# Gate and up weights of two column tiles summed and split during the out-projection, stored split in DRAM and loaded by their visits

## The chip, the cores and the metric

The kernel runs on one core of one Trainium2 chip. The metric is device microseconds of one execution; the time of a kernel is the median of several runs. A separate execution is taken with the hardware profiler, and all rows below come from that one.

## What is computed

One layer of a hybrid backbone on 1024 latent and 128 context tokens of width 1024: a mixer (differential attention, a bidirectional recurrence, a Fourier mixing) with one output projection, and then a SwiGLU feed-forward network. The part around the change is:

```python
x = x + g1 * rmsnorm(mixer_parts @ w_out, g_post_mix)
h = rmsnorm(x, g_pre_ffn) * (1.0 + sc2) + sh2
gt, up = split(h @ w_gate_up)          # two halves of 2816 columns
f = (silu(gt) * up) @ w_down
x = x + g2 * rmsnorm(f, g_post_ffn)
```

## The kernel before, in words

Every fp32 product is made of three matmuls on split operands: a high part (`copy` on ACT, L169, rounds to fp32r) and a low part (`lo` on DVE, L175, subtracts the high part). `mm3` (L185 to L187) multiplies high by low, high by high and low by high.

**Out-projection.** Nine token tiles of 128 tokens, each 12.1 us of TensorE. The loop `for t, ki in opg` (L1438) gets a turn after every second contraction step, so ki runs from 0 to 7 in a tile. After tile t come, in program order: squares of its two halves on ACT (`oproj_sq`, L1092), a reciprocal root on POOL (`rstd2`, L1083 and L1084), scaling and the residual sum on DVE (`oproj_post1`, L1098 and L1100) with squares on ACT (L1101), a second `rstd2`, and a scaling on DVE (`oproj_post2`, L1111). At ki 7 of the next tile TensorE transposes the result (`h2_turn`, L1409, tile `ot`); it stands in TensorE's queue between two tiles, so the next tile's matmuls wait for it. DVE and ACT then modulate it (`h2_mod`, L1424 and L1421, tile `ou`), split it into the operand `av` (`token_operands1`, `token_operands2`) and POOL forms sums of its quarters (`token_sums`, L1393 to L1396).

**Gate and up.** The product uses seven block products in place of eight (a Strassen scheme). A visit v is a column tile g of 128 gate and 128 up columns times one or two chunks of tokens: chunk 0 has 320 columns per matmul, chunk 1 has 256. Visits 0, 1 and 2 take tiles 0, 1 and 2 with chunk 0 alone, since chunk 1 is not ready; their chunk 1 comes in visits 6, 9 and 12. All other visits take both chunks (`VIS`, L1332). A visit has seven products of 12 matmuls per chunk. Its weights are a raw tile of 1 MB (`raw`, two buffers, `load_gu`), three sums on POOL (`weight_sums`, L1356 to L1358, into `t3`, `t2` and the raw tile), a fourth on POOL (L1374) and seven splits, one per product, by `prep(q)`: q counts products, 7 to a visit. A split goes to one of seven slots (`slots`, tile name `gu`). `prep` runs four products ahead of the product that uses it, and products 0 to 3 are prepared in the last two tiles of the out-projection.

**The order.** The order of each engine is the order of the code; the framework adds the waits. All DMAs but one are issued from SP's queue, in program order, and a DMA that waits holds back those behind it. In the gate and up stage the same queue carries the stores of hidden tiles (`HB<-hf`, L1556) and, in full visits, loads and stores of summed weights for the later stage (`tw`, `WT<-tw`, L1586 and L1596; POOL's L1593 and L1594 come just ahead of the stores).

Of the kernel before, what the change touches and what calls it, by code (L numbers as in the profile page):

```python
# [9 lines left out]
F32 = mybir.dt.float32  # L10
# [6 lines left out]
P = 128  # L17
D = 1024
# [135 lines left out]
def _body(tc, nc, A):  # L154
# [7 lines left out]
    def rdma(eng, out, in_):  # L162

        f = lambda v: v.bitcast(F32) if v.dtype == F32R else v
        eng.dma_start(f(out), f(in_))
# [28 lines left out]
    ML = tc.dram_tile([D, T], F32, name="ML")  # L194
    X1 = tc.dram_tile([T, D], F32, name="X1")
    HB = tc.dram_tile([NT, P, NJ, P], F32, name="HB")
    HS = [tc.dram_tile([8, P, NK, P], F32, name=f"HS{i}") for i in range(2)]
    WT = tc.dram_tile([NK, P, 4 * 512], F32, name="WT")
    H2B = tc.dram_tile([2, P, D], F32, name="H2B")
# [607 lines left out]
    for i in range(2, NU):  # L807
        ps = mm.tile([P, 3, 512], F32, name=f"pu{i}", tag="mm")
        w = wsl.pop(i)
# [533 lines left out]
    avp = pool("av", side="right", reuse_waits="tile")  # L1343
    AV = [[avp.tile([P, 7, 4, CN[0]], F32R, name=f"av0{h}") for h in range(2)]]

    def load_gu(v):
        SP.dma_start(raw[v % 2].rearrange("p a c -> p (a c)"), A["w_gu"][VIS[v][0]])

    PRODS = (0, 3, 1, 4, 6, 2, 5)

    def weight_sums(v):

        r = raw[v % 2]
        POOL.tensor_tensor(t3, r[:, 1, 512:], r[:, 1, :512], op=OP.subtract)  # L1356
        POOL.tensor_tensor(t2, t3, r[:, 0, :512], op=OP.add)
        POOL.tensor_tensor(r[:, 1, :512], r[:, 1, :512], r[:, 0, :512], op=OP.subtract)  # L1358

    def prep(q):  # L1360

        v, p = divmod(q, 7)
        if v >= NV_:
            return
        r = raw[v % 2]
        if q == 0:
            weight_sums(0)
        b11, b21, b12, b22 = r[:, 0, :512], r[:, 0, 512:], r[:, 1, :512], r[:, 1, 512:]
        src = (b11, t2, b21, t3, b12, b21, b22)[p]
        w = slots[q % NS]  # L1370
        copy(ACT, w[:, 0], src)
        lo(w[:, 1], src, w[:, 0])
        if p == 2:
            POOL.tensor_tensor(b21, b21, t2, op=OP.subtract)  # L1374
        elif p == 5 and v + 1 < NV_:
            weight_sums(v + 1)
        elif p == 6 and v + 2 < NV_:
            load_gu(v + 2)

    def token_split(dst, u, i, vs, src):  # L1380
        c = slice(64 * i, 64 * i + 64)
# [46 lines left out]
        SP.dma_start(H2B[t - PT[0]], hu[t].rearrange("p a k c -> p (a k c)"))  # L1428

    load_mix(2)  # L1430
    oproj_sq(0, 0)
    oproj_sq(0, 1)
    rstd2(ovec[:, 0])
# [4 lines left out]
    for t, ki in opg:  # L1438
        if ki == 6 and t + 2 < NT:
            load_mix(t + 2)  # L1440
        if t > 1 and ki == 3:
            oproj_sq(t, 0)
        if t == 2 and ki in HK0:
            h2_turn(0, HK0.index(ki))
            if ki == HK0[1]:
                h2_mod(0, 0)
                h2_mod(0, 1)
                token_operands1(AV[0], hu[0], 0)
                token_sums(hu[0])
        if (t, ki) == (2, KO2):  # L1450
            token_operands2(AV[0], hu[0], 0)
        for q in range(2):
            if t > 1 and ki == HK[q]:
                h2_turn(t - 1, q)
        if ki == 7:
            oproj_sq(t, 1)
            rstd2(ovec[:, t])
            if t > 1:
                h2_mod(t - 1, 0)
                h2_mod(t - 1, 1)  # L1460
                if PT[0] <= t - 1 < 7:
                    h2_store(t - 1)
            oproj_post1(t)
            if 2 < t < PT[0] + 2:
                token_operands2(AV[0], hu[t - 2], t - 2)
            if 1 < t <= PT[0]:
                token_operands1(AV[0], hu[t - 1], t - 1)
            oproj_post2(t)
            if 1 < t <= PT[0]:
                token_sums(hu[t - 1])  # L1470
            if t + 2 < NT:
                load_x1in(t + 2)
        if t == 6 and ki == 0:
            load_gu(0)
        if t >= 7 and ki in (2, 4) and 2 * (t - 7) + (ki == 4) < NS0:
            prep(2 * (t - 7) + (ki == 4))

# [410 lines left out]
```

## Time and profile before

| what | value |
|---|---|
| median of 3 runs (lowest to highest) | 1401.82 us (1400.85 to 1402.37) |
| the profiled execution's own time | 1395.38 us |
| its span in the profile | 1393.6 us |
| TensorE, VectorE, ScalarE, GpSimd busy share | 96%, 63%, 43%, 42% |
| mean share of the 16 DMA engines, SP's queue | 53.6% |
| transposes behind the out-projection's last tile | 638.3 us |
| visits 0, 1 and 2 | 639.1 to 689.3 us |

Starts in the trace are microseconds from the span's start. A row of the timeline gives start, duration, engine, line, operation, output and inputs, and in brackets the idle time before it with what ended it. Matmuls overlap, so their durations are longer than the distance between their starts; the distance is what counts.

### The profile page before, as it was taken

How to read it: one execution, taken by the hardware profiler on the slowest of the kernel's cores; microseconds unless marked ns; L12 is line 12 of the kernel's file. 1: busy time of each engine (PE TensorE's matmuls, PEld its weight loads, DVE VectorE, ACT ScalarE, POOL GpSimd, SP SyncE). 2: the span in 40 equal slices, each digit the busy share in tenths (PEclk: the TensorE clock that was granted, in tenths of full speed). 3: DMA queues.
4: the chain of work that ended last, by engine and by line, in shares of the span. 5: the costliest groups of instructions: out<-in, count | busy, mean ns of one | idle time of the engine just before them, and what ended most of it. 6: DMA issues, size and time to landing. Idle time of an engine off the chain costs nothing.

```text
span 1393.6 us, 22864 instructions
## 1 busy us (share of the span) xinstructions
PE 1343.8 (96%) x8786; PEld 1225.4 (88%) x8786; DVE 877.1 (63%) x1302; ACT 593.2 (43%) x1176; POOL 582.1 (42%) x523
## 2 busy tenths in 40 slices
PE   7999999998999999999899999999999999999997
PEld 6887789798898888888799999999999998888886
DVE  5824444672788872666887777767666666555564
ACT  7511226643788883546423332322222245343431
POOL 2301111230576672444766666668665532010111
PEclk9999999999999999999999999999999999999999
DMA  8567751148654525563254544557454479546564
GB/s 323 193 210 268 243 192 46 38 144 198 170 145 111 143 61 170 172 220 139 95 178 171 186 150 142 168 205 232 153 165 128 144 233 316 182 171 200 172 236 143
DMA packets 156342, 242.41 MB, mean 174 GB/s; under 512 B 9253, under 2 KB 113098, under 8 KB 152778
## 3 DMA queue, kind: packets, MB, share of 16 engines
q1 hardware_dynamic: 156090, 240.44, 53.6%
q8 instruction: 69, 1.13, 0.3%
q10 hardware_dynamic: 144, 0.52, 0.1%
q14 instruction: 39, 0.32, 0.1%
HBM read 172.62 MB, written 68.31 MB: 173 GB/s over the span
## 4 chain that ended last, share of the span: by engine, by line
PE 49%; DVE 2%; issue 1%; ACT 1%; POOL 0%; DMA 0%; DVEq 0%; POOLq 0%; ACTq 0%
PE g L187 11%; PE g L185 11%; PE g L186 11%; PE d L185 6%; PE d L187 6%; PE d L186 6%; DVE gu L175 1%; DVE av L175 0%; DVE u L1533 0%; ACT gu L169 0%; DMA raw_gu<-in_w_down 0%; DVE hf L1533 0%; ACT av L169 0%; DVE hd L175 0%; ACT hd L169 0%
## 5 line engine op out<-in xcount | busy, mean ns | idle before, releaser
L187 PE MATMUL g<-av,gu 128*128 128x320 f32 (+1 forms) x1232 | 364.2, 296 | 7.7 <-DVE gu L175 7.4
L185 PE MATMUL g<-av,gu 128*128 128x320 f32 (+1 forms) x1232 | 364.3, 296 | 1.2 <-ACT av L169 0.8
L186 PE MATMUL g<-av,gu 128*128 128x320 f32 (+1 forms) x1232 | 363.1, 295 | 0.0
L187 PEld LDWEIGHTS g<-av,gu 128*128 128x128 f32 x1232 | 232.1, 188 | 10.3 <-DVE gu L175 10.2
L185 PEld LDWEIGHTS g<-av,gu 128*128 128x128 f32 x1232 | 231.9, 188 | 2.3 <-issue 1.4
L186 PEld LDWEIGHTS g<-av,gu 128*128 128x128 f32 x1232 | 232.2, 188 | 0.0
L175 DVE TENSOR_TENSOR gu<-raw_gu,gu 128x512 fp32r<-128x512 f32 x149 | 162.6, 1104 | 36.8 <-ACT gu L169 36.8
L185 PE MATMUL pu<-hl,w 128*128 128x384 f32 x336 | 123.0, 366 | 3.3 <-POOL hl L175 2.6
L187 PE MATMUL pu<-hh,w 128*128 128x384 f32 x336 | 113.3, 337 | 0.0
L186 PE MATMUL pu<-hh,w 128*128 128x384 f32 x336 | 113.1, 337 | 0.0
L185 PE MATMUL d<-dw,hd 128*128 128x512 f32 x244 | 95.7, 392 | 0.8 <-DVE dw L175 0.8
L943 PE MATMUL s<-ks,qs 128*128 128x384 f32 x384 | 91.6, 360 | 4.5 <-DMA ks<-KL 2.6
L187 PE MATMUL d<-dw,hd 128*128 128x512 f32 x244 | 95.6, 392 | 0.0
L186 PE MATMUL d<-dw,hd 128*128 128x512 f32 x244 | 95.3, 390 | 0.0
L1533 DVE TENSOR_TENSOR u<-g,u 128x320 f32<-128x320 f32 (+1 forms) x176 | 77.1, 448 | 26.8 <-PE g L187 26.7
L949 DVE TENSOR_REDUCE nm<-s 128x1 f32<-128x1152 f32 x64 | 86.6, 1353 | 9.8 <-PE s L943 9.6
L956 ACT ACTIVATE p<-s,nm 128x1152 f32<-128x1152 f32 x64 | 78.2, 1222 | 29.2 <-DVE nm L949 16.1
L169 ACT ACTIVATE gu<-raw_gu 128x512 fp32r<-128x512 f32 x149 | 88.7, 620 | 4.5 <-DMA raw_gu<-WT 2.9
L185 PEld LDWEIGHTS pu<-hl,w 128*128 128x128 f32 x336 | 63.5, 189 | 20.4 <-issue 13.7
L997 PE MATMUL o<-av,th 128*128 128x128 f32 x576 | 79.8, 275 | 0.0
L1552 ACT ACTIVATE u<-u 128x576 f32<-128x576 f32 (+2 forms) x26 | 15.9, 612 | 143.2 <-DVE u L1533 143.2
L997 PEld LDWEIGHTS o<-av,th 128*128 128x128 f32 x576 | 73.8, 191 | 0.2
(292 smaller groups left out, 2908.7 us busy)
## 6 DMA issues: line engine op xcount, KB each, us to landing
raw_gu<-in_w_gu SPq DMA_DIRECT2D x25, 1024.0 KB, 5.0
wmb<-in_w_mod SPq DMA_DIRECT2D x32, 512.0 KB, 5.2
tw<-in_w_down SPq DMA_DIRECT2D x22, 512.0 KB, 6.0
WT<-tw SPq DMA_DIRECT2D x22, 512.0 KB, 2.7
HS<-sa SPq DMA_DIRECT2D x22, 512.0 KB, 4.0
hr<-HS SPq DMA_DIRECT2D x16, 704.0 KB, 5.0
hr<-HB SPq DMA_DIRECT2D x15, 704.0 KB, 4.2
HB<-hf SPq DMA_DIRECT2D x18, 576.0 KB, 4.5
```

Of the source, the lines that this page charges most:

```text
L169: ACT.activation(out, in_, AF.Copy)
L175: eng.tensor_tensor(out, x, hi.bitcast(F32), op=OP.subtract)
L185: PE.matmul(out, wh, xl, start=first, stop=False)
L186: PE.matmul(out, wh, xh, start=False, stop=False)
L187: PE.matmul(out, wl, xh, start=False, stop=last)
L943: PE.matmul(b[:, j, :CW], q[:, st_, m, i * P:(i + 1) * P], ks[:, m, j * CW:(j + 1) * CW], start=(st_ == 0), stop=(st_ == 1))
L949: DVE.tensor_reduce(nm, s, axis=AX.XY, op=OP.max, negate=True)
L956: ACT.activation(p.rearrange("p (n c) -> p n c", c=CW), s, AF.Exp, bias=nm, accum_out=ss)
L997: PE.matmul(d["o"], d["t", g][:, i * P:(i + 1) * P], v[:, 3 * g + i], start=(g == 0 and i == 0), stop=(g == 2 and i == 2))
L1533: add = lambda out, x: DVE.tensor_tensor(out, b, x, op=OP.add)
L1552: ACT.activation(tmp("u3"), tmp("u3"), AF.Silu)
```

## The change

The sums and splits of column tiles 0 and 1 are made once, in the out-projection. A generator `early_gen` is advanced at ki 1, 3 and 5 of tiles 2 to 8: one step makes the three sums, each of the next seven makes one split into slot 2 or 3 by turns and stores it (512 KB) to a new DRAM tensor `WP`; with the seventh split of tile 0 the raw tile is loaded again, for column tile 1. The 17th step, in tile 7, loads the raw weights of the first visit that still splits. In visits 0, 1, 6 and 9 `prep` is a load of 512 KB from `WP` into the slot; the other visits are as before.

```diff
+    WP = tc.dram_tile([2, 7, P, D], F32, name="WP")
...
-    def load_gu(v):
-        SP.dma_start(raw[v % 2].rearrange("p a c -> p (a c)"), A["w_gu"][VIS[v][0]])
+    NPRE = 2
+    REAL = [v for v in range(NV_) if VIS[v][0] >= NPRE]
+
+    def load_raw_gu(r, g):
+        SP.dma_start(r.rearrange("p a c -> p (a c)"), A["w_gu"][g])
+
+    def load_gu(i):
+        if i < len(REAL):
+            load_raw_gu(raw[i % 2], VIS[REAL[i]][0])
...
+    def split_gu(r, p, w):
         b11, b21, b12, b22 = r[:, 0, :512], r[:, 0, 512:], r[:, 1, :512], r[:, 1, 512:]
         src = (b11, t2, b21, t3, b12, b21, b22)[p]
-        w = slots[q % NS]
         copy(ACT, w[:, 0], src)
         lo(w[:, 1], src, w[:, 0])
         if p == 2:
             POOL.tensor_tensor(b21, b21, t2, op=OP.subtract)
-        elif p == 5 and v + 1 < NV_:
-            weight_sums(v + 1)
-        elif p == 6 and v + 2 < NV_:
-            load_gu(v + 2)
+
+    def prep(q):
+        v, p = divmod(q, 7)
+        if v >= NV_:
+            return
+        w, g = slots[q % NS], VIS[v][0]
+        if g < NPRE:
+            rdma(SP, w, WP[g, p].rearrange("p (a c) -> p a c", a=2))
+        else:
+            i = REAL.index(v)
+            split_gu(raw[i % 2], p, w)
+            if p == 6:
+                load_gu(i + 2)
+        if p == 5 and v + 1 in REAL:
+            weight_sums(raw[REAL.index(v + 1) % 2])
+
+    def early_gen():
+        for g in range(NPRE):
+            weight_sums(raw[0])
+            yield
+            for p in range(7):
+                w = slots[2 + p % 2]
+                split_gu(raw[0], p, w)
+                rdma(SP, WP[g, p].rearrange("p (a c) -> p a c", a=2), w)
+                if p == 6 and g + 1 < NPRE:
+                    load_raw_gu(raw[0], g + 1)
+                yield
+        load_gu(0)
+        yield
...
     load_mix(2)
+    load_raw_gu(raw[0], 0)
+    early = early_gen()
...
-        if t == 6 and ki == 0:
-            load_gu(0)
+        if t > 1 and ki in (1, 3, 5):
+            next(early, None)
         if t >= 7 and ki in (2, 4) and 2 * (t - 7) + (ki == 4) < NS0:
             prep(2 * (t - 7) + (ki == 4))
```

What the diff does not show is where the new instructions fall among those of the out-projection. Three places matter. In the rows the lines are those of each kernel's own file (a line of the new kernel stands one to some thirty lines further down), and a name's first number is the token tile or the slot.

First ACT in tile 3, before, from the squares of tile 3's first half:

```order
L1092 ACTIVATE tm3_6072,ovec_3334<-op30_6046 128x512
L1092 ACTIVATE tm3_6072,ovec_3334<-op31_6047 128x512
L1421 ACTIVATE ou2_6115<-ot21_6107,M_83,S2_85 128x2x64
L1421 ACTIVATE ou2_6115<-ot21_6107,M_83,S2_85 128x2x64 x3
L1101 ACTIVATE tm3_6072,ovec_3334<-x13_5916 128x512
```

and now:

```order
L169 ACTIVATE gu2_5841<-raw_gu0_5836 128x512
L1093 ACTIVATE tm3_6087,ovec_3335<-op30_6057 128x512
L169 ACTIVATE gu3_5842<-t3_5838 128x512
L169 ACTIVATE gu2_5841<-raw_gu0_5836 128x512
L1093 ACTIVATE tm3_6087,ovec_3335<-op31_6058 128x512
L1448 ACTIVATE ou2_6136<-ot21_6128,M_84,S2_86 128x2x64
```

The second copy into slot `gu2` stands ahead of the squares of tile 3's second half (`op31`), and it may start only when the store of what the first copy and its DVE row left in `gu2` has landed. Tiles 5 and 6 have the same pattern.

Second POOL in tile 4, before:

```order
L1395 TENSOR_TENSOR ou2_6115<-ou2_6115 128x256
L1396 TENSOR_TENSOR ou2_6115<-ou2_6115 128x256
L1083 TENSOR_SCALAR ovec_3334<-ovec_3334 128x1
L1084 TENSOR_TENSOR ovec_3334<-ovec_3334,mhalf_82 128x1
L1083 TENSOR_SCALAR ovec_3334<-ovec_3334 128x1
```

and now:

```order
L1422 TENSOR_TENSOR ou2_6136<-ou2_6136 128x256
L1423 TENSOR_TENSOR ou2_6136<-ou2_6136 128x256
L1365 TENSOR_TENSOR t3_5838<-raw_gu0_5836 128x512
L1366 TENSOR_TENSOR t2_5837<-t3_5838,raw_gu0_5836 128x512
L1367 TENSOR_TENSOR raw_gu0_5836<-raw_gu0_5836 128x512
L1084 TENSOR_SCALAR ovec_3335<-ovec_3335 128x1
L1085 TENSOR_TENSOR ovec_3335<-ovec_3335,mhalf_83 128x1
```

The three sums of column tile 1 have come between the sums of token tile 2 and the first `rstd2` of tile 4 (`ovec`); they wait for the raw tile, whose load SP issues behind the stores of the sixth and seventh split.

Third SP around the end of visit 5, before:

```order
L1347 DMA raw_gu1_6640<-in_w_gu 128x2048
L1596 DMA WT_74<-tw20_7598 128x1024
L1596 DMA WT_74<-tw21_7599 128x1024
L1556 DMA HB_71<-hf5_7665 128x9x128
```

and now:

```order
L165 DMA gu2_5841<-WP_72 128x1024
L1625 DMA WT_75<-tw20_7627 128x1024
L1625 DMA WT_75<-tw21_7628 128x1024
L165 DMA gu3_5842<-WP_72 128x1024
L1585 DMA HB_71<-hf5_7691 128x9x128
L165 DMA gu4_6682<-WP_72 128x1024
```

The loads of the fourth split (`gu3`) and of those after it in visit 6 stand behind the stores of `WT` and of `HB`. Visit 9 has the same order behind visit 8.

## Rows read from the trace of the kernel before

**Rows 1.** The page: busy us of each engine, share of the span, instructions.

```profile
PE 1343.8 (96%) x8786; PEld 1225.4 (88%) x8786; DVE 877.1 (63%) x1302; ACT 593.2 (43%) x1176; POOL 582.1 (42%) x523
```

**Rows 2.** Windows, visits 0, 1, 2, 5: PE, PEld, DVE, ACT, POOL busy; clock; DMA.

```profile
639.10:652.49 13.39, 13.39 (x95) 13.27 (x94) 7.92 (x14) 9.81 (x24) 6.51 (x9) 1.00 0.58 209
652.49:671.73 19.24, 14.31 (x87) 12.36 (x86) 15.75 (x20) 10.27 (x23) 15.26 (x12) 1.00 0.14 42
671.73:689.32 17.59, 13.76 (x87) 12.34 (x86) 15.38 (x21) 7.63 (x16) 14.17 (x12) 1.00 0.32 110
733.00:755.00 22.00, 22.00 (x169) 22.00 (x168) 14.44 (x22) 5.61 (x11) 13.95 (x10) 1.00 0.49 172
```

**Rows 3.** Waits of TensorE in visits 0 to 2: total us, times, longest.

```profile
PE g L187 <- DVE gu L175: 7.4, 6, 2.2
```

**Rows 4.** Timeline of TensorE: first matmuls of products 1 and 2.

```profile
640.94 0.31 PE L185 MATMUL g<-av,gu 128*128 128x320 f32 x1
...
642.70 0.31 PE L185 MATMUL g<-av,gu 128*128 128x320 f32 x1
```

**Rows 5.** The raw tile's instructions: shortest, median, longest ns, starts.

```profile
L169 ACT ACTIVATE gu<-raw_gu x149: 613/618/636, 620.6 to 1336.5; 128x512 fp32r<-128x512 f32 x149
L175 DVE TENSOR_TENSOR gu<-raw_gu,gu x149: 673/693/1837, 624.7 to 1340.3; 128x512 fp32r<-128x512 f32 x149
...
L1356 POOL TENSOR_TENSOR t<-raw_gu x25: 1294/1737/2348, 620.7 to 1097.8; 128x512 f32<-128x512 f32 x25
...
L1374 POOL TENSOR_TENSOR raw_gu<-raw_gu,t x25: 1288/1294/1728, 634.6 to 1114.9; 128x512 f32<-128x512 f32 x25
```

**Rows 6.** Timeline of TensorE: transposes behind tiles 3 and 4.

```profile
577.88 1.04 PE L1409 MATMUL ot<-ident,tm 128*128 128x128 f32 x8
...
589.96 1.04 PE L1409 MATMUL ot<-ident,tm 128*128 128x128 f32 x8
```

**Rows 7.** Timeline of DVE in the out-projection, tiles 2 and 3.

```profile
576.30 1.36 DVE L1111 TENSOR_SCALAR tm<-x,ovec 128x512 f32<-128x512 f32 x2
578.51 1.37 DVE L1424 TENSOR_SCALAR ou<-ot,S,M 128x128 f32<-128x128 f32 x4 [0.85 <-PE ot L1409]
580.85 0.75 DVE L1098 SCALAR_TENSOR_TENSOR tm<-op,ovec,G 128x512 f32<-128x512 f32 x1 [0.96 <-POOL ovec L1084]
...
587.53 1.36 DVE L1111 TENSOR_SCALAR tm<-x,ovec 128x512 f32<-128x512 f32 x2
```

**Rows 8.** Timeline of POOL: the first `rstd2` of tile 4.

```profile
591.09 0.30 POOL L1083 TENSOR_SCALAR ovec<-ovec 128x1 f32<-128x1 f32 x1
591.48 0.56 POOL L1084 TENSOR_TENSOR ovec<-ovec,mhalf 128x1 f32<-128x1 f32 x1
```

**Rows 9.** Timeline of ACT: squares of tile 3's second half.

```profile
578.08 0.60 ACT L1092 ACTIVATE tm<-op 128x512 f32<-128x512 f32 x1 [1.87 <-PE op L187]
```

**Rows 10.** DMA issues of 570 to 640 us: KB each, median us to landing.

```profile
X<-x SPq DMA_DIRECT2D x6, 512.0 KB, 3.7
x<-in_x SPq DMA_DIRECT2D x5, 512.0 KB, 3.3
...
mtl<-ML SPq DMA_DIRECT2D x4, 512.0 KB, 7.0
raw_gu<-in_w_gu SPq DMA_DIRECT2D x2, 1024.0 KB, 5.2
H2B<-ou SPq DMA_DIRECT2D x2, 512.0 KB, 2.6
...
ub<-H2B SPq DMA_DIRECT2D x1, 512.0 KB, 5.2
```

**Rows 11.** The raw tile's loads over the whole span.

```profile
DMA to landing us min/median/max: 3.5/5.5/10.0
```

**Rows 12.** Timeline of SP's queue at the end of visit 5.

```profile
757.88 2.10 SPq L1596 DMA_DIRECT2D WT<-tw  x2
760.03 0.43 SPq L1556 DMA_DIRECT2D HB<-hf  x1
```

**Rows 13.** Timeline of TensorE: visit 6's fourth product begins.

```profile
760.62 0.28 PE L185 MATMUL g<-av,gu 128*128 128x256 f32 x1
```

More of the change, by code (lines that the diff above doesn't have):

```diff
@@ L1344, in _body, with weight_sums @@
     AV = [[avp.tile([P, 7, 4, CN[0]], F32R, name=f"av0{h}") for h in range(2)]]
-    def load_gu(v):
-        SP.dma_start(raw[v % 2].rearrange("p a c -> p (a c)"), A["w_gu"][VIS[v][0]])
+    NPRE = 2
[5 more added lines that the diff above has]
+            load_raw_gu(raw[i % 2], VIS[REAL[i]][0])
     PRODS = (0, 3, 1, 4, 6, 2, 5)
-    def weight_sums(v):
-        r = raw[v % 2]
+    def weight_sums(r):
         POOL.tensor_tensor(t3, r[:, 1, 512:], r[:, 1, :512], op=OP.subtract)
@@ L1358, in weight_sums @@
         POOL.tensor_tensor(r[:, 1, :512], r[:, 1, :512], r[:, 0, :512], op=OP.subtract)
+    def split_gu(r, p, w):
+        b11, b21, b12, b22 = r[:, 0, :512], r[:, 0, 512:], r[:, 1, :512], r[:, 1, 512:]
+        src = (b11, t2, b21, t3, b12, b21, b22)[p]
+        copy(ACT, w[:, 0], src)
+        lo(w[:, 1], src, w[:, 0])
+        if p == 2:
+            POOL.tensor_tensor(b21, b21, t2, op=OP.subtract)
     def prep(q):
@@ L1364, in prep @@
             return
[L1365 to L1369, printed above, removed]
-        w = slots[q % NS]
[L1371 to L1374, printed above, removed]
-        elif p == 5 and v + 1 < NV_:
-            weight_sums(v + 1)
-        elif p == 6 and v + 2 < NV_:
-            load_gu(v + 2)
+        w, g = slots[q % NS], VIS[v][0]
[21 more added lines that the diff above has]
+        yield
     def token_split(dst, u, i, vs, src):
```

## The prediction

> **What bounds the kernel now.** I read the page first: TensorE is busy for 1343.8 of 1393.6 us [rows 1], so little is to be won but at the places where it waits. Windows cut at the visits' first matmuls find one such place. A product of 12 matmuls takes 1.76 us on chunk 0, the distance of two neighbouring product starts [rows 4], so a visit of seven takes 12.3 us. Visit 0 took 13.4 us, of which some 0.8 us are transposes of the last token tile; visit 1 took 19.2, visit 2 took 17.6 us, and visit 5 ran with TensorE full [rows 2]. Visits 1 and 2 therefore lost 6.9 and 5.2 us, 12.1 together with hardly anything in visit 0. The waits name the low parts of the weights on DVE as what came last, 7.4 us in six waits [rows 3]; the rest is in short gaps. The windows also say why: in those two visits DVE is busy for 31 of 37 us and POOL for 29 [rows 2], since the second token chunk is made ready there too, and a low part that takes 0.69 us at the median takes up to 1.84 us [rows 5].
>
> Then the out-projection, where the new work goes. TensorE has no gap there, but it waits in order: a tile takes 12.1 us from one group of transposes to the next [rows 6], and the group behind tile t+1 needs tile t's second scaling on DVE. Behind tile 3 that scaling ended at 577.66 (576.30 and 1.36) and the transposes began at 577.88; behind tile 4 it ended at 588.89, for 589.96 [rows 6, 7]. So the chain of one tile through ACT, POOL and DVE has 0.2 to 1.1 us to spare, though no engine of it is full.
>
> **What the change does, part by part.**
>
> *Removed from visits 0 and 1:* 14 copies on ACT, 14 low parts on DVE and eight sums on POOL; with the four sums and seven splits of visit 1 gone, what visit 1 lost goes as well. In visit 2 the splits stay, but the queues ahead of them are emptier; a low part is made four products (7 us) ahead. I take 3 of its 5.2 us as won, and 10 us in all, between 7 (nothing in visit 2) and 12. The same removal in visits 6 and 9 wins nothing, because TensorE was full there, as in visit 5 [rows 2].
>
> *Added, tile 2 of the out-projection.* Three sums now stand before the token sums of tile 0 on POOL, one copy before the squares of tile 2 on ACT, one low part before the modulation on DVE. The copy costs 0.6 and the low part 0.7 us in line [rows 5], the sums up to a microsecond more. With 0.2 us to spare I take 1.2 us, between 0.5 and 2.
>
> *Added, tiles 3, 5 and 6: the wait for a slot.* Three splits per tile share two slots. The third split's copy waits on ACT until the first split's store has landed, and the squares of the tile's second half (0.60 us, [rows 9]) stand behind that copy. The first split's low part comes after the previous tile's second scaling on DVE. That closes a loop from one second scaling to the next: low part 0.7, store 3.7 to landing as for the X store [rows 10], third copy 0.6, its low part 0.7, modulation 1.4 (1.37, [rows 7]), which makes 7.1 us; then the old stretch from the first scaling to the end of the second, 580.85 to 588.89, 8.0 us [rows 7]. That is 15.1 us against a tile of 12.1, and TensorE waits 3.0 us at the transposes. In tile 5 a sum on POOL (1.3, [rows 5]) stands before `rstd2` (0.9, [rows 8]) behind the third low part in place of the modulation: 15.9, so 3.8 us. Tile 6 has one operand split in place of three on DVE, some 0.9 us less, so 2.1 us. Together 8.9 us.
>
> *Added, tile 4: the wait for the raw tile.* The reload for column tile 1 is issued after the low parts of the sixth and seventh split. They follow the second scaling of tile 3: two low parts 1.4 and issue 0.4, landing 5.2 [rows 10], three sums 4.4 (1.29 to 1.74 each, [rows 5]), `rstd2` 0.9 [rows 8], and again 8.0 to the next second scaling. 20.3 against 12.1: TensorE waits 8.2 us behind tile 5. This is the largest single term. Before, `rstd2` of tile 4 ran at 591.09, as soon as POOL was done with the token sums [rows 8].
>
> *SP's queue in the out-projection.* The operands of tile t+2 are now issued behind the stores of that tile's splits, up to 5.8 us after the second scaling, and take 7.0 us to land [rows 10]. At 12.8 us they are hidden by the loop of 15.1 us; without that loop they would cost about 0.7 us. The 14 extra stores and 4 early loads are hidden otherwise.
>
> So the out-projection gets 1.2 + 8.9 + 8.2 = 18.3 us longer. The bounds: stores landing as fast as those of H2B (2.6) and the raw tile in 3.5 us [rows 10, 11], sums at their fastest and tile 2 at its least give 12. All slow together (two low parts per loop at 1.84 us, the raw tile in 10.0 us [rows 5, 11]) gives 34.
>
> *Added, visits 6 and 9: loads behind stores.* The load for product 3 of visit 6 stands in SP's queue behind both stores of WT. The second left at 759.98 (757.88 and 2.10, [rows 12]); the product began at 760.62 [rows 13]. The load is of the size and shape of a load of x, 3.3 us; that of `ub` took 5.2 [rows 10]. So it lands between 763.3 and 765.2 and the product waits 2.7 to 4.6 us. I take 3.5; the later loads then follow in step. In the early visits the same loads have room: the queue is short and slots are free three products ahead. Visit 9 repeats visit 6, so 7.0 us, 5.4 to 9.2.
>
> **The sum.** 18.3 - 10 + 7.0 = +15.3 us. The profiled execution took 1395.38 us, which is 6.4 below the median of the runs, 1401.82; the sum makes 1410.7 of the one and **1417** of the other, and the median is what I predict.
>
> **The rivals.**
>
> *Faster, by the waits of visits 1 and 2.* If stores and reload landed early enough for the chain to stay within a tile, 10 us would be won: 1392. For tile 3 that needs a store landed 0.7 us after its issue, and visit 6 needs a load in 0.6; nothing here lands in under 2.6 [rows 10]. It decides as soon as the out-projection's waits and the late loads together stay below 7 us. Chance 0.06, and 0.05 for a sum that ends near nothing.
>
> *Loads of visits 6 and 9 in time, the rest as forecast.* Without their 7.0 us the time is 1410. For it: POOL has less to do around them. Against it: the sums ahead of the WT stores are those of visit 5, which stay. Chance 0.12.
>
> *The splits and sums get in each other's way.* Low parts beside POOL's sums took up to 1.84 us in place of 0.69, and a sum up to 2.35 in place of 1.29 [rows 5]. If in each of four loops both low parts are slow, 9 us come on top: 1426, and up to 1431 with a slow raw tile. The Trainium skill, "SBUF — State Buffer", section "Who interferes with whom", has a rule for it: a DVE instruction with two SBUF inputs and a GpSimd instruction that reads SBUF exclude each other, and the later one is blocked until the first is done. By that rule the moved low parts would often wait out a whole sum. The longest rows agree, the median does not, because POOL is idle for much of a tile. Chance 0.12.
>
> *The change does not do what it says:* visits 1 and 2 stay bound by token operands and sums, and only 4 us come back: 1423. Chance 0.07.
>
> **How the numbers follow.** The forecast has 0.58, from 1406 (the low bound of the out-projection, 12, less 12, plus 5.4, so +5) to 1424. Loads in time lie inside that, slow splits reach to 1431, and so I take 1406 to 1431. What a measurement here can tell from no change is about 0.2%, 2.8 us. Faster by more has 0.06, within it 0.05, slower 0.89.
>
> **What would show it.** Right: in the new profile TensorE waits at the transposes behind tiles 3 to 7, some 8 us behind tile 5 and 2 to 4 us behind tiles 4, 6 and 7; ACT waits for DMA before a copy into a slot in tiles 3, 5 and 6, and POOL for a DMA before the sums in tile 4. Visits 0 to 2 last about 40 us in place of 50.2, and visits 6 and 9 each have one wait for a load from WP. Wrong: transposes without a wait would break the largest term, visits 1 and 2 at 17 us or more the gain, and visits 6 and 9 without a wait the last term.

## The result, and the profile after

The changed kernel takes 1436.4 us (median of four runs, 1432.6 to 1444.5) against 1402.1 for the kernel before (four runs): 1.026 times as long, with a 95% interval of 1.0227 to 1.0294. It is slower, as forecast, but by 34 us and not by 15, outside the range of 1406 to 1431.

The page of the changed kernel, the busy line that answers to [rows 1]:

```profile
PE 1355.1 (95%) x8786; PEld 1235.5 (86%) x8786; DVE 861.6 (60%) x1288; ACT 585.8 (41%) x1162; POOL 563.0 (39%) x515
```

DVE, ACT and POOL have less to do by 7 to 19 us each, as the change promised. TensorE has the same 8786 matmuls and is busy 11 us longer: part of them ran at the lower clock. The other 26 us of the span (1430.6 against 1393.6) are waits.

Windows of the changed kernel, the first five cut at the transposes behind tiles 2 to 7 of the out-projection, the last three at visits 0, 1 and 2 (columns as in [rows 2]):

```profile
563.28:577.42 14.14, 12.24 (x58) 9.73 (x56) 8.59 (x17) 7.48 (x19) 6.01 (x9) 1.00 0.68 207
577.42:595.59 18.17, 12.50 (x57) 9.75 (x57) 10.39 (x17) 8.05 (x20) 6.81 (x10) 0.97 0.67 216
595.59:618.60 23.01, 14.84 (x57) 11.77 (x57) 9.77 (x16) 6.60 (x17) 9.32 (x12) 0.80 0.56 182
618.60:635.31 16.71, 13.69 (x57) 10.95 (x57) 10.47 (x17) 7.44 (x18) 6.82 (x10) 0.91 0.69 221
635.31:649.93 14.62, 13.85 (x57) 11.08 (x57) 9.43 (x15) 6.76 (x17) 5.07 (x8) 0.88 0.76 253
...
662.83:681.58 18.75, 15.58 (x95) 14.84 (x94) 8.22 (x15) 10.45 (x27) 4.65 (x8) 0.91 1.03 422
681.58:696.56 14.98, 12.57 (x87) 12.34 (x85) 9.78 (x17) 6.07 (x13) 10.65 (x10) 1.00 0.56 194
696.56:710.17 13.61, 12.85 (x87) 12.33 (x86) 11.40 (x13) 5.97 (x12) 12.20 (x11) 1.00 0.14 35
```

A tile took 12.1 us before, the distance of the two groups in [rows 6]; now five tiles in a row take 14.1, 18.2, 23.0, 16.7 and 14.6. Visit 2 is better by 4.0 us and visit 1 by 4.3, but visit 0, which was as good as full before [rows 2], takes 5.4 us longer while the DMA engines are busy all of the time at 422 GB/s.

The changed kernel's timeline of TensorE, transposes behind tiles 3 to 6:

```profile
577.42 0.63 PE L1436 MATMUL ot<-ident,tm 128*128 128x128 f32 x4 [1.90 <-DVE tm L1112]
...
595.59 1.94 PE L1436 MATMUL ot<-ident,tm 128*128 128x128 f32 x8 [5.52 <-DVE tm L1112]
618.60 1.94 PE L1436 MATMUL ot<-ident,tm 128*128 128x128 f32 x8 [8.17 <-DVE tm L1112]
635.31 1.94 PE L1436 MATMUL ot<-ident,tm 128*128 128x128 f32 x8 [3.02 <-DVE tm L1112]
```

Before there was no wait in them [rows 6]. What the second scaling waits for in its turn stands on ACT and POOL (timelines of the changed kernel, the longest of each):

```profile
585.73 0.63 ACT L169 ACTIVATE gu<-raw_gu 128x512 fp32r<-128x512 f32 x1 [8.00 <-DMA WP<-gu]
```

```profile
606.45 1.28 POOL L1365 TENSOR_TENSOR t<-raw_gu 128x512 f32<-128x512 f32 x1 [7.28 <-DMA raw_gu<-in_w_gu]
```

These are the slot's wait and the reload's wait of the prediction. SP's queue and TensorE at visit 6 answer to [rows 12, 13]:

```profile
778.26 2.09 SPq L1625 DMA_DIRECT2D WT<-tw  x2
780.40 0.42 SPq L165 DMA_DIRECT2D gu<-WP  x1
```

```profile
785.62 0.55 PE L185 MATMUL g<-av,gu 128*128 128x256 f32 x1 [3.97 <-DMA gu<-WP]
786.39 0.41 PE L185 MATMUL g<-av,gu 128*128 128x256 f32 x1
...
788.56 0.51 PE L185 MATMUL g<-av,gu 128*128 128x256 f32 x1
```

The product waits 3.97 us for a load behind the stores of `WT`, and its twelve matmuls then take 2.94 us in place of 1.41.

For the accounts below the span is cut in three stages: **A**, from the transposes behind tile 2 to those behind tile 8; **B**, from there to the end of the last DVE multiplication of visit 5; **C**, from there to that of visit 10, so with visits 6 and 9. Between the profiled executions before and after, A went from 72.5 to 98.8 us (+26.3), B from 120.2 to 116.8 (-3.3), C from 86.5 to 100.5 (+14.0); -2.5 lies ahead of A, where only a raw load and the first early steps of tile 2 are new, and +2.6 behind C. The sum is the 37.0 us between the spans.

Stages are safer to compare than whole times here: in executions of versions whose work ahead of it is the same, stage A began anywhere from 563.3 to 573.2 us. That is as much as some edits are worth. Stages vary too where they have long waits: A took 98.8, 101.3, 97.6 and 99.8 us in the change and in the three versions with the same early steps in tiles 2 to 6 (raw loads later, loads ahead of HB, HB behind the loads). Without the long waits it took 79.6 to 79.8 in four versions, and C took 86.5 wherever visits 6 and 9 split raw tiles. Each stage time is that of one profiled execution.

| version | ratio to before (95%) | A | B | C |
|---|---|---|---|---|
| before | 1 | 72.5 | 120.2 | 86.5 |
| the change | 1.0260 (1.0227-1.0294) | 98.8 | 116.8 | 100.5 |
| four slots | 1.0216 (1.0188-1.0243) | 89.8 | 119.0 | 100.6 |
| sums later | 1.0219 (1.0189-1.0248) | 90.0 | 118.2 | 102.5 |
| both | 1.0207 (1.0182-1.0233) | 79.6 | 126.1 | 102.4 |
| clock filler | 1.0266 (1.0225-1.0308) | 97.7 | 117.6 | 100.8 |
| both, no early sums | 1.0144 (1.0115-1.0173) | 77.7 | 124.2 | 98.3 |
| raw loads later | 1.0263 (1.0240-1.0286) | 101.3 | 115.8 | 99.5 |
| and loads ahead of HB | 1.0240 (1.0211-1.0269) | 97.6 | 115.2 | 100.4 |
| and HB behind the loads | 1.0250 (1.0222-1.0278) | 99.8 | 116.6 | 100.6 |
| both, raw later, ahead of WT | 1.0141 (1.0117-1.0165) | 79.7 | 123.5 | 94.2 |
| the same from tile 1 | 1.0133 (1.0110-1.0155) | 82.9 | 116.7 | 94.1 |
| both, 6 and 9 from raw, from tile 1 | 1.0079 (1.0052-1.0106) | 82.8 | 118.9 | 86.5 |
| two tiles, all that helped | 1.0079 (1.0053-1.0106) | 79.8 | 124.7 | 86.5 |
| the same, 11 of 14 loads halved | 1.0064 (1.0039-1.0089) | 79.7 | 122.5 | 86.5 |
| visit 1 alone | 0.9989 (0.9971-1.0007) | 75.7 | 114.4 | 86.5 |
| visit 1, its loads first | 0.9996 (0.9981-1.0012) | 75.7 | 114.4 | 86.5 |

In the two versions that start in tile 1, 2.4 and 1.7 us more lie just ahead of A, in the distance of the transposes before it (10.2 and 9.5 for 7.9 us).

### The profile page after: what moved, and what is told of

Same layout as the page of the kernel before. It is cut to its first block, busy times and chain, and to the rows that moved or that the text cites. A ratio compares the mean times of both kernels' runs of the same rounds, so it can differ in the third digit from the quotient of the medians.

```text
span 1430.6 us, 22897 instructions
## 1 busy us (share of the span) xinstructions
PE 1355.1 (95%) x8786; PEld 1235.5 (86%) x8786; DVE 861.6 (60%) x1288; ACT 585.8 (41%) x1162; POOL 563.0 (39%) x515
## 4 chain that ended last, share of the span: by engine, by line
PE 64%; DVE 9%; DMA 7%; ACT 6%; POOL 5%; issue 3%; SPq 1%; DVEq 0%; POOLq 0%; ACTq 0%
PE g L185 10%; PE g L187 10%; PE g L186 10%; PE d L185 6%; PE d L187 6%; PE d L186 6%; PE pu L185 3%; PE pu L187 2%; PE pu L186 2%; PE s L944 2%; PE o L998 2%; DMA gu<-WP 1%; PE t L983 1%; ACT p L957 1%; POOL wt L976 1%
## 5 line engine op out<-in xcount | busy, mean ns | idle before, releaser
L185 PEld LDWEIGHTS g<-av,gu 128*128 128x128 f32 x1232 | 234.3, 190 | 16.1 <-issue 8.7
L187 PEld LDWEIGHTS g<-av,gu 128*128 128x128 f32 x1232 | 234.4, 190 | 1.7 <-DVE gu L175 1.7
L186 PEld LDWEIGHTS g<-av,gu 128*128 128x128 f32 x1232 | 234.7, 191 | 0.0
L175 DVE TENSOR_TENSOR gu<-raw_gu,gu 128x512 fp32r<-128x512 f32 x139 | 148.8, 1083 | 44.7 <-ACT gu L169 44.7
L169 ACT ACTIVATE gu<-raw_gu 128x512 fp32r<-128x512 f32 x139 | 82.8, 619 | 24.3 <-DMA WP<-gu 20.0
L1581 ACT ACTIVATE u<-u 128x576 f32<-128x576 f32 (+2 forms) x26 | 15.9, 613 | 162.3 <-DVE u L1562 162.3
L185 PEld LDWEIGHTS pu<-hl,w 128*128 128x128 f32 x336 | 63.0, 188 | 20.3 <-issue 13.6
L998 PE MATMUL o<-av,th 128*128 128x128 f32 x576 | 79.8, 275 | 0.0
```

What stands on the lines that cost most here:

```text
L169: ACT.activation(out, in_, AF.Copy)
L175: eng.tensor_tensor(out, x, hi.bitcast(F32), op=OP.subtract)
L185: PE.matmul(out, wh, xl, start=first, stop=False)
L186: PE.matmul(out, wh, xh, start=False, stop=False)
L187: PE.matmul(out, wl, xh, start=False, stop=last)
L998: PE.matmul(d["o"], d["t", g][:, i * P:(i + 1) * P], v[:, 3 * g + i], start=(g == 0 and i == 0), stop=(g == 2 and i == 2))
```

## The experiments

**The out-projection: slots.**

```
-                w = slots[2 + p % 2]
+                w = slots[p % 4]
```

> The early splits go round four staging slots in place of two, so that no third split of a tile waits for the first one's store. Theory (chain with landings: in tiles 3, 5 and 6 the loop from one second scaling to the next, 18.2, 16.7 and 14.6 us, is set by the store's landing): these loops go back to about 12.1 us, the loop of tile 4 (23.0 us, set by the raw tile's reload) stays within 2 us; the out-projection, 98.8 us in the changed kernel from the first transposes to the end of the last, takes 86 to 89, and the time falls by 10 to 13 us to about 1425. Rival (the added copies, low parts and sums slow ACT, DVE and POOL themselves, the slots do not matter): the loops of tiles 3, 5 and 6 stay over 15 us and the time falls by less than 4.

Stage A fell by 8.9 us to 89.8, a little less than expected (a tile is counted from the transposes behind it to the next ones). Tiles 3, 5 and 6 come to 13.7, 13.8 and 12.5 us, and tile 4 takes 23.7. So the slots were the cause of most of what those three had over 12.1, 9.5 of 13.2 us. By the ratios the time fell by some 6 us only, short of the 10 to 13 expected, and their intervals overlap; B grew by 2.1.

**The out-projection: the reload.**

```
                     load_raw_gu(raw[0], g + 1)
+                    yield
+                    yield
```

> The three sums of column tile 1 come two steps of the early work later, behind the operands of tile 4 on POOL, so that nothing of tile 4 stands behind the wait for the reloaded raw tile. Theory (chain with landings): the loop of tile 4, 23.0 us, goes back to about 12.1 us; the slot waits stay, in tiles 3, 6 and 7 by the new order; the time falls by 8 to 12 us, to 1425 to 1428. Rival (POOL is short of time for the sums, wherever they stand): the wait moves to another tile, one loop stays over 18 us, and the time falls by less than 4.

8.7 us less in A: tile 4 takes 13.7 us, and the slot waits are in tiles 3, 6 and 7 now (17.9, 14.8 and 16.0). Here too the ratios give some 6 us, for 8 to 12 expected.

**Both.**

> Both together, four slots and the sums two steps later. Theory (chain with landings): all loops are within 1.5 us of 12.1, TensorE waits less than 4 us in all at the transposes, the out-projection takes 73 to 77 us (72.5 before the change), and the time falls by 20 to 25 us to 1412 to 1416: still 10 to 14 above the kernel before, which visits 6 and 9 account for (13.6 us, less the 2.9 won in visits 0 to 2). Rival (work itself too much for ACT, DVE and POOL in a tile): out-projection over 82 us, time above 1420.

A fell by 19.1 us, a little more than the two added up, but to 79.6 and not to 73 to 77: 7.1 us are left, 2.0 in tile 2, 1.9 in tile 3, 2.6 in tile 5 and 0.5 in tile 6. TensorE waits 2.8 us for scalings. And by the ratios the time fell by some 7 us only, because B grew by 9.3: with two steps more, the early work ends in tile 8, and the loads of visit 0's first products are issued behind it (TensorE waits 3.7 and 6.3 us for two of them). In A, DVE and POOL slow each other. This version's DVE in tile 3, three low parts of the early work, and POOL beside them:

```profile
582.47 1.21 DVE L175 TENSOR_TENSOR gu<-raw_gu,gu 128x512 fp32r<-128x512 f32 x1
583.61 1.22 DVE L175 TENSOR_TENSOR gu<-t,gu 128x512 fp32r<-128x512 f32 x1
584.75 1.21 DVE L175 TENSOR_TENSOR gu<-raw_gu,gu 128x512 fp32r<-128x512 f32 x1
...
588.05 0.75 DVE L1099 SCALAR_TENSOR_TENSOR tm<-op,ovec,G 128x512 f32<-128x512 f32 x1 [0.81 <-POOL ovec L1085]
```

```profile
583.22 1.06 POOL L1424 TENSOR_TENSOR ou<-ou 128x256 f32<-128x256 f32 x1
584.36 1.06 POOL L1425 TENSOR_TENSOR ou<-ou 128x256 f32<-128x256 f32 x1
585.38 1.72 POOL L1376 TENSOR_TENSOR raw_gu<-raw_gu,t 128x512 f32<-128x512 f32 x1
587.07 0.30 POOL L1084 TENSOR_SCALAR ovec<-ovec 128x1 f32<-128x1 f32 x1
```

A low part takes 1.21 us and not 0.69 [rows 5], a token sum 1.06 and not 0.74, and the fourth weight sum of 1.72 us stands ahead of `rstd2`, for which DVE then waits. But TensorE does not wait for this: the transposes behind tile 4, at 595.85, follow without a gap. The windows of tiles 2 and 3 show what costs time there:

```profile
567.73:581.83 14.10, 12.23 (x57) 9.73 (x56) 8.56 (x17) 7.47 (x19) 5.98 (x9) 1.00 0.69 209
581.83:595.85 14.02, 13.87 (x57) 10.98 (x58) 11.40 (x17) 7.75 (x19) 7.64 (x10) 0.88 0.84 270
```

Tile 2 waits, 1.86 us at the transposes behind it; in tile 3 TensorE is full, but at a granted clock of 0.88.

**Both, without the early sums.** The splits take the raw blocks, the four sums of an early column tile are left out:

```
-            weight_sums(raw[0])
...
-        src = (b11, t2, b21, t3, b12, b21, b22)[p]
+        src = (b11, t2 if sums else b12, b21, t3 if sums else b22, b12, b21, b22)[p]
```

> The version with four slots and later sums, without the four sums of each early column tile on POOL: the splits take the raw quarter blocks in place of the summed ones, so the weights of visits 0 and 1 are other ones. What is left in the out-projection are the copies, low parts, stores and reload. Its out-projection took 79.6 us, 7.1 over the kernel before, with low parts of 1.2 us beside POOL's work. Theory (sums in line on POOL, and low parts slowed beside them): 73 to 76 us. Rival (the copies and low parts themselves fill the chain): 78 or more.

77.7, between the two. Tiles 2 to 4 take 12.1, 12.6 and 12.5 us where they took 14.1, 14.0 and 12.1, so in tile 2 the sums were all of it. How they did it stands on DVE: they start beside the second scaling of tile 1. The version with the sums (DVE, then POOL), the one without, and the kernel before:

```profile
562.31 2.94 DVE L1112 TENSOR_SCALAR tm<-x,ovec 128x512 f32<-128x512 f32 x2 [1.83 <-POOL ovec L1085]
```

```profile
562.24 1.29 POOL L1365 TENSOR_TENSOR t<-raw_gu 128x512 f32<-128x512 f32 x1
563.62 1.35 POOL L1366 TENSOR_TENSOR t<-t,raw_gu 128x512 f32<-128x512 f32 x1
```

```profile
561.65 0.88 DVE L1112 TENSOR_SCALAR tm<-x,ovec 128x512 f32<-128x512 f32 x2 [1.83 <-POOL ovec L1085]
```

```profile
560.40 0.88 DVE L1111 TENSOR_SCALAR tm<-x,ovec 128x512 f32<-128x512 f32 x2 [1.84 <-POOL ovec L1084]
```

Two scalings take 2.94 us in place of 0.88 and end 0.28 us behind the second sum, and that is the 2.0 us of tile 2; the copy and the low part, which the version without sums keeps, cost nothing there. In the change itself the pair takes 2.95. Without that wait the clock stays at 1.00 in tile 3. Tile 5 takes 16.2: TensorE waits for its operands, which SP issues behind the early stores, and then runs at a clock of 0.89 over the tile, which costs another 2 us.

```profile
606.62 0.50 PE L185 MATMUL op<-wol,mth 128*128 128x512 f32 x1 [1.28 <-DMA mth<-MH]
608.17 0.52 PE L187 MATMUL op<-woh,mtl 128*128 128x512 f32 x1 [0.82 <-DMA mtl<-ML]
```

These lines have their own lateness: in the version with both edits the same two waits are 0.22 and 0.80.

**Is the low clock behind the waits a cost of its own?** After the waits of tiles 4 to 6 the granted clock is 0.80, 0.91 and 0.88 in the windows above (and 0.50, 0.70 and 0.66 in the 5 us from the transposes on, where I wrote 0.58 to 0.66 below).

```
+    FILL = {4: 20, 5: 31, 6: 10}
...
+        for _ in range(FILL.get(t, 0) if ki == 7 else 0):
+            PE.matmul(flb, woh[:, 0, 0:P], woh[:, 0, 0:512], start=True, stop=True)
```

> The changed kernel with 20, 31 and 10 matmuls whose result nobody uses, put on TensorE ahead of the waiting transposes in tiles 4, 5 and 6, to fill most of the waits of 5.5, 8.2 and 3.0 us and so keep the granted clock up behind them (it was 0.58 to 0.66 in the 5 us behind each wait). Theory (the loop on ACT, DVE and POOL sets the out-projection, the slow matmuls behind a wait are hidden in the next wait): clock near 1.0 in the out-projection, waits longer by what the matmuls are faster, time the same within 2 us. Rival (the low clock is a cost of its own, 98.8 - 72.5 = 26.3 us less 19.4 us of waits): the time falls by 5 to 8 us.

A is 97.7 us, 1.1 less, within what A varies by. The window of the slowest tile in this version:

```profile
603.39:626.50 23.11, 19.50 (x89) 15.54 (x87) 9.58 (x16) 6.39 (x16) 9.16 (x12) 1.00 0.56 182
```

Its clock is 1.00 for 0.80, and the tile takes 23.1 us as before. The rival falls: in tiles 4 to 6 of the change the loop through ACT, DVE and POOL sets the time and hides the clock. Where the loops are gone it is not hidden: with four slots alone, tile 3 has TensorE busy throughout, at a clock of 0.88:

```profile
583.48:597.19 13.71, 13.71 (x57) 11.14 (x58) 11.07 (x17) 7.75 (x19) 7.37 (x10) 0.88 0.85 270
```

**The late visits.** Two ways to free visits 6 and 9. The first issues their loads up to six products ahead, ahead of the `WT` stores; the same run moves two raw loads:

```
-                while nprep <= q + LEADQ:
+                while nprep <= q + LEADQ or nprep <= q + 6 and nprep // 7 in (6, 9):
...
+                if q in (2, 8):
+                    load_gu(q // 8)
```

> On the version with four slots and later sums, two edits in two stages. (a) The raw loads of visits 2 and 3 (1 MB each) are issued behind the third and ninth product of the visits and no longer ahead of the loads from WP. Measured from the last transposes of the out-projection to the last DVE multiplication of visit 5: 120.2 us before the change, 116.8 with it, 126.1 in the version that this one edits. Theory (too much is loaded at once in visit 0, and in a poor order: WP loads, raw tiles, G, X, H2B share full DMA engines): 126.1 falls by 8 or more, to 110 to 118. Rival (the WP loads alone are too much or are issued too late for their slots): over 122. (b) In visits 6 and 9 the WP loads are issued six products ahead in place of four, so that those of products 3 and 4 stand ahead of the WT stores in SP's queue. Measured over visits 6 and 7 together, and 9 and 10: 32.2 and 32.2 before, 40.5 and 40.1 in the edited version. Theory (loads behind stores): at most 34.5 each. Rival (the slots of the loads come free too late, or DMA too slow): over 37.

Visits 6 and 7 take 35.3 us, between the two expectations; 9 and 10 take 37.1, the rival's number. The waits come later and are shorter (5.2 us in three for loads, where the change has 7.5 in two), since only two more loads fit ahead of the stores. The second way splits in 6 and 9 as before the change, and starts the early work a step earlier:

```
-    REAL = [v for v in range(NV_) if VIS[v][0] >= NPRE]
+    REAL = [v for v in range(NV_) if v >= NPRE]
...
-        if t > 1 and ki in (1, 3, 5):
+        if t > 0 and ki in (1, 3, 5):
```

> On the version with four slots and later sums: visits 6 and 9 take their raw tiles and split them again as before the change, only visits 0 and 1 read WP; and the early work begins one step earlier, in tile 1. Theory: visits 6 and 7 together, and 9 and 10, go back to 32.2 us each within 0.5 (40.5 and 40.1 in the edited version), since they lost nothing by their own splits before; the out-projection stays within 3 us of the edited version's 79.6; visits 0 to 5 come down from 126.1 us if the late end of the early work held up the first loads there (to 118 or less), and stay if not. Time about 1405 to 1412. Rival (the traffic of WP delays whatever else is loaded): visits 6 and 9 stay over 34.

32.16 us each, exactly as before the change: all 14.0 us of stage C come from loading in these two visits. B came down from 126.1 to 118.9, near the 118 expected where the late end of the early work was in the way; A is 3.2 us longer.

> All of it together: four slots, sums two steps later, early work from tile 1, raw loads of visits 2 and 3 later, loads of visits 6 and 9 ahead of the WT stores. If the stages add: out-projection 77 to 82 us (72.5 before), visits 0 to 5 110 to 114 (120.2), visits 6, 7, 9 and 10 66 to 69 in all (64.4): within 5 us of the kernel before, on either side. If the loads of visits 0 and 1 stay late whatever stands ahead of them, 8 to 15 us slower than before.

With 82.9, 116.7 and 94.1 it is 1.0133 times before: all three stages missed what was expected, on the slow side, and with some 19 us over before it is slower than both cases named.

**The early visits.** First, on the change itself, only the raw loads of visits 2 and 3 moved behind the third and ninth product:

> The changed kernel with one edit: the raw loads of visits 2 and 3 are issued behind the third and ninth product of the visits, no longer ahead of the loads from WP. Theory (the early visits won 2.9 us and not 10 because the raw loads and the WP loads share the DMA engines in visit 0): from the last transposes of the out-projection to the last DVE multiplication of visit 5 it takes 108 to 112 us in place of 116.8, and the out-projection stays at 98 to 99. Rival (WP loads are late by themselves, for slots or for their own amount): 115 to 117.

115.8: my theory falls. Visit 0 lost less (15.6 us for 18.8), but visit 1 now waits 3.48 us for a load that stands behind the HB store in SP's queue. Windows of this version, visit 0, and visit 1 up to the product that waits:

```profile
672.75:688.32 15.57, 13.70 (x95) 13.19 (x93) 6.32 (x12) 8.55 (x22) 4.67 (x8) 1.00 1.02 421
688.32:699.09 10.77, 7.29 (x48) 7.05 (x49) 6.63 (x11) 5.01 (x12) 6.56 (x7) 0.96 0.56 189
```

So visit 1's loads were put ahead (`nprep // 7 in (1,)` in the line shown above for visits 6 and 9), and then the HB store behind all of them:

> The version with the raw loads later, and the loads of visit 1 issued up to six products ahead, so that those of products 4 and 5 stand ahead of the HB store of visit 0, which holds SP's queue for 9.2 us while the DMA engines idle. In the version that this one edits, visit 1 lost 6.4 us to one late load and the slow matmuls behind it. Theory (head of the queue): the stretch from the end of the out-projection to the end of visit 5 takes 108 to 112 us, in place of 115.8. Rival (the amount of WP traffic is what makes loads late): over 114.

> The changed kernel with raw loads later and visit 1's loads up to six products ahead, and now the HB store of visit 0 behind all of visit 1's loads too. In the version that this one edits the load of visit 1's last product still stood behind that store and cost 3.9 us with the slow matmuls after it. Theory (the WP loads can be in time when nothing stands ahead of them): the stretch from the end of the out-projection to the end of visit 5 falls from 115.2 to 111 to 112 us (120.2 before the change). Rival (a load elsewhere becomes late, since the total is too much for the time): 114 or more.

115.2 and 116.6: the rival's numbers. In the first of the two, TensorE still waits 2.7 us for loads; the second falls short by another mechanism than the rival's. In it TensorE does not wait for a load from WP in visits 0 to 2 at all. Visits 0 and 1 together take 27.3 us where the change has 33.7, and visit 2 takes 20.2 where it has 13.6. The loss has moved. Its visit 2:

```profile
699.53:719.73 20.20, 15.13 (x85) 13.96 (x86) 17.99 (x23) 8.05 (x16) 15.67 (x14) 0.92 0.18 56
```

**One column tile only.** Eight early steps, two a tile in tiles 2 to 5, for visit 1's column tile, whose loads are issued up to six products ahead; the rest as before the change:

```
-    REAL = [v for v in range(NV_) if VIS[v][0] >= NPRE]
+    REAL = [v for v in range(NV_) if v != 1]
...
-        if t > 1 and ki in (1, 3, 5):
+        if t > 1 and ki in (1, 5):
```

> Only the column tile of visit 1, the one that lost most before, is split early: three sums and seven splits in tiles 2 to 5, two steps a tile, four slots, no reload in between; visits 0, 6 and 9 split from raw tiles as before the change; the loads for visit 1 are issued up to six products ahead, so that all but the last stand ahead of visit 0's HB store. Theory (what the change wins is in visits 1 and 2, what it loses is in slot and reload waits, crowded tiles, crowded loads in visit 0 and late loads in 6 and 9): the out-projection takes 74 to 78 us (72.5 before, 98.8 changed), the stretch from there to the end of visit 5's last DVE multiplication 108 to 113 (120.2 and 116.8), visits 6, 7, 9 and 10 as before; 3 to 9 us faster than before the change. Rival (any split in the out-projection costs what a split in a visit saves): no faster than before, within 3 us or slower.

In this version the down projection's first loads overwrite the last visit's raw tile, so its hidden values are others; the instructions are the same. Stage A, 75.7, is as expected; B, 114.4, is not (108 to 113), and by its time the version can't be told from the kernel before. The next version has the raw buffers exchanged and the loads put in order:

```
-            if p == 6:
+            if p == 6 and v:
                 load_gu(i + 2)
...
+                if q == 7:
+                    SP.dma_start(*held.pop())
+                    load_gu(2)
```

> As the version that splits only the column tile of visit 1 early, with two loads put in order: the raw tile of visit 3 (1 MB, whose issue waited for visit 0's last split ahead of visit 1's six loads) and the HB store of visit 0 are issued behind all loads of visit 1; and the two raw buffers change places in the down projection's first loads, since the number of raw tiles is now odd. There, 2.8 us went at the first product of visit 1 to a load issued at 654.0. Theory (head of SP's queue): that wait goes, the stretch from the end of the out-projection to the end of visit 5 falls from 114.5 us to 110 to 112, the out-projection stays at 75 to 77, and the kernel is 3 to 7 us faster than before the change. Rival (slots or the amount loaded): the stretch stays at 114 or more and the time is within 3 us of before.

The wait at visit 1's first product is gone and B is 114.4: nothing is won. Windows of visits 0, 1 and 2 in this version, and TensorE's waits in them:

```profile
646.63:660.02 13.39, 13.39 (x96) 13.28 (x95) 7.84 (x14) 9.65 (x24) 5.38 (x8) 1.00 0.96 359
660.02:672.34 12.32, 12.32 (x87) 12.26 (x85) 7.07 (x12) 6.45 (x16) 7.77 (x8) 1.00 0.66 223
672.34:691.11 18.77, 13.66 (x87) 12.39 (x85) 16.56 (x21) 7.68 (x16) 14.32 (x13) 1.00 0.12 33
```

```profile
PE g L187 <- DVE gu L175: 3.2, 2, 2.2
PE g L185 <- DVE u L1561: 1.9, 2, 1.2
```

Visit 1 is full, and visit 2 loses 6.4 us (18.77 less 12.33), more than the 5.2 before: DVE is busy for 16.6 of 18.8 us with its own splits and the token operands. In visits 0 and 1 it is busy for 7.8 of 13.4 and 7.1 of 12.3 us, so it has time there; the code only places visit 2's work later. No run moved that work forward. This version, at 0.9996, neither beats the kernel before nor loses to it: +3.2 in A and -5.7 in B are the limit of what was found here (1.7 of the 3.2 lie in tile 2, where the sums again hold the scalings up, 2.9 us for 0.88; no run moved them off), and 2.5 us is about what this measurement can tell.

**Two tiles with all that helped, and the same with the high parts alone of most loads** (`rdma(SP, w[:, 0], WP[g, p, :, :512])`).

> Two column tiles as in the change, with all that has helped: four slots, later sums, later raw loads, visit 1's loads ahead of the HB store, visits 6 and 9 split from raw tiles. If the stages add: out-projection 79.7 us (72.5 before), stretch to the end of visit 5 115 to 119 where the late end of the early work still holds up the first loads (120.2 before), or 108 to 112 where the HB store was what counted; visits 6, 7, 9 and 10 as before. So between 4 us faster and 7 us slower than before the change.

> The version with two column tiles and all that helped, but of 11 of the 14 weight tiles of visits 0 and 1 only the high parts are loaded from WP (256 KB in place of 512): the low parts are left out, so 2.9 of 7.3 MB are not moved. Theory (in visit 0 the DMA engines are full, and loads land after 8 us in place of 3 to 4): landings of the WP loads at the median 6 us or less, and the stretch from the end of the out-projection to the end of visit 5 is 3 us or more shorter than with full loads. Rival (late issue, not the amount): within 1 us of it.

1.0079: A at 79.8 and C as before, B at 124.7, where the second and third product of visit 0 wait 3.7 and 3.3 us for late loads. With two fifths of the bytes left out B comes down by 2.2 us, short of the 3 expected; the halved loads land after 6.2 us at the median, for 8.9 (7.9 for the three full ones). The amount matters; the late issue matters more (with all else the same, the start in tile 1 brought B from 123.5 to 116.7).

## Why the prediction was right and wrong

**The waits of slots and raw tile (8.9 and 8.2): right in place, too small.** They show at the places named. Taking each away gave 8.9 and 8.7 us, and both together 19.1. But in the change each loop was longer than forecast (18.2 for 15.1 in tile 3, 23.0 for 20.3 in tile 4, 16.7 for 15.9, 14.6 for 14.2), 7.0 us in all, and these are most of the 8 us by which the out-projection was missed. The terms that were too small are the landings: the store issued at 579.74 let ACT go at 585.73, 6.0 us for my 3.7, and the reload took 7.4 us for 5.2. Two low parts in tile 4, beside token sums, took 2.35 for 1.4. That TensorE's largest wait, 8.17 us behind tile 5, equals my 8.2 is luck: the loop was 10.9 us longer than a tile before, and at the clock of 0.80 the matmuls filled 2.7 us of that.

**"Added, tile 2 of the out-projection ... I take 1.2 us": this step failed.** Tile 2 cost 2.0 us, and not by what I priced: the copy and the low part cost nothing, and the sums cost it through DVE, by holding up the scalings beside them. I had counted added work only on its own engine. I had also priced it in tile 2 alone. With neither wait left, the new work still cost 7.1 us: the 2.0, then 1.9 in tile 3 at the clock behind tile 2's wait, and 3.1 in tiles 5 and 6. Of these, 1.0 is for operands that SP issues behind the stores ("without that loop they would cost about 0.7 us").

**The rival of splits and sums in each other's way (0.12) was in part the truth.** Low parts in the out-projection of the version with both edits took 1.21 us, 1.75 times 0.69. By the Trainium skill, "SBUF — State Buffer", section "Who interferes with whom", the later of two such instructions, a low part with two SBUF inputs and a sum on GpSimd, waits out the earlier whole one. The rows agree, as far as POOL's rough spans go. From 583.68 to 585.96 low parts and token sums end by turns (583.68, 584.28, 584.83, 585.42, 585.96), each 0.54 to 0.60 us behind the end of the other engine's instruction, where it takes 0.69 or 0.74 alone. The scalings beside the weight sums do the same: the pair ends 0.28 us behind the end of the second sum. So the mechanism of this rival was there, but the time that it cost TensorE came from scalings, which it did not name.

**"In the early visits the same loads have room: the queue is short and slots are free three products ahead": this step failed.** In visit 0 the DMA engines were busy throughout at 422 GB/s, and the 14 loads from WP took 9.4 us at the median to land:

```profile
gu<-WP SPq DMA_DIRECT2D x14, 512.0 KB, 9.4
```

TensorE waited for three of them in visit 0 and one in visit 1, 5.6 us in all. The product behind the first wait took 2.94 us for 1.76 and the next one 2.70 (0.32 of it a wait), at granted clocks of 0.59 and 0.81. My durations came from a stretch with far less traffic [rows 10].

**"I take 3 of its 5.2 us as won, and 10 us in all": this step failed too, and by itself.** Even where no load is late, the three visits take 44.5 us (one column tile) or 47.5 (two), not 40. In visit 2 its own splits and the second chunk's token operands keep DVE and POOL busy. Where TensorE waits for loads in visits 0 and 1, those engines catch up, and visit 2 is short: 12.3 us in the version with raw loads later, after 34.4 for the first two. Where the loads are in time, it is 18.8 or 20.2. I had read the two visits as two losses with separate causes; what the first no longer loses, the second does. My rival that visits 1 and 2 "stay bound by token operands and sums" (0.07) had this mechanism: 5.7 and 2.7 us come back, for its 4. That DVE and POOL set the sum is read from the windows, waits and the moved loss, and is not shown: no run took token work away, or moved visit 2's splits into the time that DVE has left in visit 1.

**Visits 6 and 9: the wait right, its price wrong.** 3.97 and 3.49 us for the load, 3.5 forecast; but stage C grew by 14.0, not 7. Behind each wait the clock was low (0.64 from 786 to 790 us, between the levels of 1.2 and 2.4 GHz):

```profile
786.00:790.00 4.00, 3.96 (x23) 3.69 (x23) 1.02 (x2) 0.00 (x0) 0.00 (x0) 0.64 1.05 416
```

In visit 6 one product took 2.94 us for 1.41; in visit 9 three took 2.91, 2.70 and 2.56, the first with a wait of 1.25 for a late low part. Visit 6 lost 5.9 us in all and visit 9 7.6. TensorE is full there, so nothing hides this, unlike in tiles 4 to 6 of the out-projection. "The later loads then follow in step" left out the clock.

**The sum.** Out-projection +26.3 for 18.3, early visits -3.3 for -10, late visits +14.0 for +7.0. All three errors have one sign. The bounds of 12 to 34 held the first; the other two lay outside theirs, and so did the time. The upper bounds of the three, 34, -7 and 9.2, add up to 1438, above the 1431 that was taken as the end of the range. That the change is slower, and that the out-projection is the largest part, was right.

## What to carry to other kernels

Work moved into a stage where no engine is full can still land on a chain with no slack: price every instruction that comes to stand in that chain, in each round, at the duration that it has beside its new neighbours, and its neighbours on other engines at the duration that they have beside it. Price a transfer at the traffic that the change itself makes, and what waits for it at the clock that follows a wait if nothing else hides it. Where two neighbouring stretches wait for the same engines, relieving the first moves the loss into the second: ask what the sum over both can become.

## What had not been expected of the hardware

Two scalings of 0.88 us took 2.94 beside two weight sums on another engine, and the sums hardly got longer (1.29 and 1.35 us, for 1.29 at the shortest before). A 512 KB load landed after 4.7 us at the median where seven were issued some 2 us apart (visit 1, its loads first, 630 to 720 us), after 7.2 where six of the seven were issued within 3 us (visit 1 alone), and after 9.4 in the change with 14; the engines moved up to 438 GB/s then. The same low granted clock was free in tiles 4 to 6 of the out-projection, and cost some 1.5 us in visit 6, 2.5 in visit 9 and 1.6 in a tile without a wait behind it. And the executions differ by up to 10 us in when stage A begins.
